# Adding the squares of the mixers' outputs by DMA, moving the first stores to another queue, and reordering ScalarE between two phases

## The chip, the cores and the metric

The kernel runs on one core of a Trainium2 chip. The metric is the device time of one execution in microseconds (us); the median of three runs before the change is 2104.57 us (2098.55 to 2105.23). The engines are called here TensorE (PE in the profile; PEld is its weight load), VectorE (DVE), ScalarE (ACT), GpSimd (POOL) and SyncE (SP). SP and POOL are used mostly to issue DMAs, each on a queue of its own.

## The reference

One step of a hybrid decoder layer in fp32: 2048 prompt tokens and 8 x 4 sample tokens, model width 1024. Cut to what matters:

```
xn   = rms_norm(x, g_mix);  proj = xn @ w_in            # pool 256 | rnn 512 | gate 512 | q 256
o_pool = pool_mixer(...)    o_rnn = gelu(gate) * rg_lru(conv(rnn), ...)    o_xa = cross_attn(q, mk, mv)
mix  = concat(group_rms(o_pool), group_rms(o_rnn), group_rms(o_xa)) * g_out
x    = x + mix @ w_out
x    = x + (gelu(conv(rms_norm(x) @ w_gate)) * (rms_norm(x) @ w_up)) @ w_down
y    = rms_norm(x, g_final)

def group_rms(x):                # over the columns of one mixer's output, for each token
    return x * rsqrt(mean(x * x, -1) + EPS)
```

The change touches how `mean(x * x)` of the three mixers' outputs is formed, where the normalised first tokens are kept for later use, and the first steps of `mix @ w_out`.

## The kernel before, in words

**Layout.** Channels lie on the 128 partitions and tokens along the free dimension. The 2080 tokens are cut into six column sets (`s` = 0 to 5) of 344 or 348 tokens; set 0 holds the sample tokens first. Two sets make a block (`b` = 0 to 2). A product in fp32 quality is made of three matmuls: each operand is split into a high and a low part (`split`, L122 and L123: ScalarE copies the high part, VectorE subtracts it).

**First phase (0 to about 250 us).** For each set the recurrent mixer runs. `g_prep` loads the x columns (L259), scales and splits them (L127, L128) into pairs of tiles `ahr`, `alr`; `g_norm` adds their squares for the token norm; `proj2` (L234) projects; then convolution (L552, L555), gates (`pg` L474, tanh L477), scan (L580), the product with the gate `g` (L597). `g_mix` (L327 on) then normalises the result: ScalarE squares it (L329), `fold` (L352) adds its chunks of 128 channels, TensorE sums the columns with a vector of ones (`rms_stat`, L164, tile `sto`), VectorE takes the reciprocal root (`rsqrt`, L150 to L155), TensorE broadcasts it (L312, tile `bco`), VectorE multiplies (L337) and POOL stores (L339).

**Second phase (about 250 to 504 us).** The same split columns are loaded back from `xhl` (L272) for the pooling and attention mixers of each set. These also end in `g_mix`, with two chunks instead of four (tiles `stp`, `bcp` and `stx`, `bcx`). Behind them the output projection of block 0 begins (`po`).

**Keeping the split columns.** With `keep` given, `g_prep` stores each finished pair to `xhl[s]` in DRAM on POOL's queue (L264). Sets 0 to 5 all use it in the kernel before.

**Squares by DMA.** `fold` and `squares` can add by VectorE or by accumulating DMAs on POOL's queue: `G.dma_start(out=q[:, 0:m], in_=q[:, m:2m], accum_op=ALU.add)`. Before the change only the token norm of sets 1 to 5 (`g_norm`, `dma=s > 0`) takes the DMAs: three in a chain, the first L363 and two of L350, tile `sqr`; their column sum is the tile `str`.

**What sets the order.** The instructions of TensorE and SP run in the order in which the program writes them. Background work (`g_prep`, `g_norm`, `g_mix`, the gates, attention) is written as generators; a planner, `Weave`, lets a clock advance by a fixed cost for each group of matmuls (0.45 for three of them in `proj2`) and takes the next step of a generator when its due time has come. The due times come from the table `W`: in `g_mix` the column sums are written `2.0 + mw * nch` units after the squares, where `mw` is `sq_r`, `sq_p` or `sq_x` and `nch` the number of chunks, and `sq_5` for the last set of the recurrent mixer. In the two first phases VectorE's, ScalarE's and POOL's orders are chosen by the framework; from the passage on they are as written.

**The passage (about 485 to 535 us)** leads to the third phase, in which all products (output projection of blocks 1 and 2, and the gated FFN) are made by a scheme with seven products of half-size pieces for eight. `B0` is the first block's pieces: `B0.hi(i)` and `B0.lo(i)` split piece i (L995, L999). `D[0][s]` are the first pair of outputs, slots s = 0 and 1; `do("hi5", s)` and `do("lo5", s)` split the weights of product 5 (L1055, L1059), `sigma1` adds two raw weight pieces (L1044), `product(0, s, B0)` runs twelve matmuls (L1074), and `post(0, n)` copies the result on ScalarE into another PSUM bank (L1084), on which product 5 goes on adding. TensorE's order of products is 0, 5, 2, 1, 3, 6, 4, each for both slots.

**Third phase (about 535 us to the end).** The change does not touch it.

Of the kernel before, what the change touches and what calls it, by code (L numbers as in the profile page):

```python
# [8 lines left out]
F32 = mybir.dt.float32  # L9
# [7 lines left out]
KD = 8  # L17
# [8 lines left out]
NCOL = [344, 344, 348, 348, 348, 348]  # L26
TOK = [(86, 4)] * 2 + [(116, 3)] * 4
COFF = [0, 344, 688, 1036, 1384, 1732]
NS = 6
# [14 lines left out]
def hybrid_kernel(ctx: ExitStack, tc: tile.TileContext, I, O):  # L44
    nc = tc.nc
# [10 lines left out]

    W = dict(pool_0=12.8, attn_0=1.42, soft0_0=9.0, st_p0=18.9, st_x5=13.5,
             norm_0=9.35, stat_0=2.55, norm_1=17.0, stat_1=4.5, prep_m=2.07, kv=11.0, gate=8.2, norm=20.0, stat=8.5, prep_r=9.7, mix_r=10.2,
             sq_r=1.6, st_r=22.5, mix_5=14.0, sq_5=1.4, st_5=7.0, bc_p=1.0, attn=0.42, soft0=8.5,
             soft1=2.0, soft2=8.5, pv=2.94, pool=10.3, sq_p=1.23, st_p=13.5, sq_x=1.16, st_x=10.5, dq=6.65,  # L60
             dsoft=5.95, dpv=7.01, dout=1.5, mix0=1.19, g2=1.4)

    class Weave:
# [40 lines left out]
    pv = cp.tile([P, NPC], F32, name="pv")  # L104
# [11 lines left out]
    def pcol(name, j):  # L116
        return pv[:, PC[name] + j:PC[name] + j + 1]
# [7 lines left out]
    def split_g(hi, lo, src, g):  # L125

        S.activation(out=hi, in_=src, func=AF.Copy, scale=g)  # L127
        V.scalar_tensor_tensor(out=lo, in0=src, scalar=g, in1=hi.bitcast(F32), op0=ALU.mult, op1=ALU.subtract)  # L128
# [61 lines left out]
    xhl = [dr.tile([P, 2, 8, n], F32, name=f"xhl{s}") for s, n in enumerate(NCOL)]  # L190
# [4 lines left out]
    def x_src(s):  # L195
        return xs[:, COFF[s] * 8:(COFF[s] + NCOL[s]) * 8].rearrange("p (k t) -> p k t", k=8)
# [23 lines left out]
    def big(shape, name):  # L220
        return yp.tile(shape, F32, tag="yh", bufs=2, name=name)
# [4 lines left out]
    def pair(name, n):  # L226

        return [ap.tile([P, 2, n], F32R, tag=t, bufs=8, name=t + name) for t in ("ah", "al")]
# [22 lines left out]
    def g_prep(st, src, n, g, name, parts=2, wait=1.2, keep=None):  # L251

        x = big([P, 8, n], "x" + name)
        st += [x, [pair(f"{name}{k}", n) for k in range(KD // 2)]]
        w = KD // parts
        for k in range(KD):
            if k == 0 or (parts > 2 and k % w == 0):
                for h in range(k, k + w if parts > 2 else KD, w):
                    nc.sync.dma_start(out=x[:, h:h + w, :], in_=src[:, h:h + w, :])  # L259
            hi, lo = (z[:, k % 2, :] for z in st[1][k // 2])  # L260
            split_g(hi, lo, x[:, k, :], pcol(g, k))
            if k % 2 and keep is not None:
                for i in range(2):
                    G.dma_start(out=keep[:, i, k - 1:k + 1], in_=st[1][k // 2][i].bitcast(F32))  # L264
            yield 0.0, wait

    def load_parts(s):

        x = [pair(f"p{s}{k}", NCOL[s]) for k in range(KD // 2)]
        for k in range(KD // 2):  # L270
            for i in range(2):
                nc.sync.dma_start(out=x[k][i].bitcast(F32), in_=xhl[s][:, i, 2 * k:2 * k + 2])  # L272
        return [None, x]
# [30 lines left out]
    def g_stat(sq_list, one, tj, J, rs, name, sd):  # L304

        rms_stat([sq_list], one, tj, J, psC("st" + name), rs, name)
        yield 0.18 * J * len(sq_list), sd

    def g_bcast(rs, n, tj, J, rb, name):
        st = psC("bc" + name)  # L310
        for j in range(J):
            T.transpose(st[:, j * tj:(j + 1) * tj], rs[:tj, j:j + 1].to_broadcast([tj, P]), ident[:tj, :tj])  # L312
        S.activation(out=rb, in_=st[:, 0:n], func=AF.Copy)
        yield 0.1 * J, 1.0
# [10 lines left out]
    def g_mix(o, nch, sqn, one, s, dst, g0, name, mw, sd):  # L325

        n = NCOL[s]  # L327
        tj, J = TOK[s]
        S.activation(out=sqn, in_=o, func=AF.Square)  # L329
        l = fold(sqn, nch)  # L330
        yield 0.0, 2.0 + mw * nch
        rs = cp.tile([P, 8], F32, tag="rs", bufs=2, name="rs" + name)
        yield from g_stat(l, one, tj, J, rs, name, sd)
        rb = kp.tile([P, n], F32, tag="rb2", bufs=1, name="rb" + name)
        yield from g_bcast(rs, n, tj, J, rb, name)
        for c in range(nch):
            V.scalar_tensor_tensor(out=o[:, c, :], in0=o[:, c, :], scalar=pcol("g_out", g0 + c), in1=rb,  # L337
                                   op0=ALU.mult, op1=ALU.mult)
        G.dma_start(out=dst, in_=o)  # L339
# [5 lines left out]
    def fold(q, m, dma=False):  # L345

        while m > 1:
            m //= 2
            if dma:
                G.dma_start(out=q[:, 0:m, :], in_=q[:, m:2 * m, :], accum_op=ALU.add, max_dma_last_dim=8192)  # L350
                continue
            V.tensor_tensor(out=q[:, 0:m, :], in0=q[:, 0:m, :], in1=q[:, m:2 * m, :], op=ALU.add)  # L352
        return [q[:, 0, :]]
# [65 lines left out]
    xq = {0: []}  # L419
    wr = [[]]  # L420
    g = g_load_w(wr[0], I["w_in"][2], "wr0", "a", 2)
    next(g)
    for k, _ in enumerate(g_prep(xq[0], x_src(0), NCOL[0], "g_mix", "r0", 4, keep=xhl[0])):
        if k == 1:
            next(g)
    wv.add(g_norm(xq[0][0], 0, "r0"))
# [77 lines left out]
    for s in range(NS):  # L504
        n = NCOL[s]
        dec = s == 0
# [3 lines left out]
        x = xq.pop(s)  # L510
# [75 lines left out]
        if dec:  # L586
            hs = kp.tile([P, 4, NB], F32, name="hs")
            V.tensor_copy(hs, xc[:, :, 0:ND].rearrange("p c (b t) -> p c b t", t=NT)[:, :, :, NT - 1])
            G.dma_start(out=O["h_s"], in_=hs.rearrange("p c b -> p (c b)"))
            G.dma_start(out=O["conv_s"], in_=xrd.rearrange("p c b t -> p (c b t)"))  # L590
        if s == NS - 1:
            cpo = kp.tile([P, 4, 3], F32, name="cpo")
            for c2 in range(2):
                V.tensor_copy(cpo[:, 2 * c2:2 * c2 + 2, :], xr_prev[c2])
            G.dma_start(out=O["h_p"], in_=h_prev)
            G.dma_start(out=O["conv_p"], in_=cpo.rearrange("p c t -> p (c t)"))
        V.tensor_tensor(out=g, in0=g, in1=xc, op=ALU.mult)  # L597
        wv.add(g_mix(g, 4, xc, 1, s, mix_r[b][:, :, hb, :], 2, f"o{s}",
                     *((W["sq_5"], W["st_5"]) if s == NS - 1 else (W["sq_r"], W["st_r"]))),
               W["mix_5"] if s == NS - 1 else W["mix_r"])  # L600


    x = load_parts(0)
# [18 lines left out]
    def g_pool(s, n, npr, p0, df):  # L622
        b, hb = divmod(s, 2)
        op = tmp("ox", [P, 2, n], f"op{s}")
        for ch in range(2):
            pP = psC(f"pP{s}{ch}")
            T.matmul(pP[:, 0:n], bdp[:, ch, :], df[:, ch, :], start=True, stop=True)
            S.activation(out=op[:, ch, :], in_=pP[:, 0:n], func=AF.Copy, scale=pcol("pscale", ch))
            yield 0.6, 0.0
        yield from g_mix(op, 2, tmp("t", [P, 2, n], f"sqp{s}"), 2, s, mix_p[b][:, 0:2, hb, :], 0, f"p{s}", W["sq_p"], W["st_p" if s else "st_p0"])  # L630
# [23 lines left out]
    def g_attn(s, n, npr, p0, qd, qs):  # L654
# [63 lines left out]
        if p0:  # L718
            yield from g_dec(qd, ox)
        yield from g_mix(ox, 2, tmp("t", [P, 2, n], f"sqx{s}"), 2, s, mix_p[b][:, 2:4, hb, :], 6, f"x{s}", W["sq_x"], W["st_x" if s < NS - 1 else "st_x5"])  # L720

    def g_dec(qd, ox):
# [54 lines left out]
    for s in range(NS):  # L777
        n = NCOL[s]
        tj, J = TOK[s]
        dec = s == 0  # L780
        p0 = ND if dec else 0
        npr = n - p0
        if s:
            x = xq.pop(s)
# [326 lines left out]
    D = []  # L1111
# [191 lines left out]
    def prod(x):  # L1303
        d, y = divmod(x, 14)
        return D[d][y % 2], order[d][y // 2], y % 2
# [90 lines left out]
    B0 = blks[0] = Block("s0", NCOL[2 * stages[0][1]], stages[0][4])  # L1396
# [46 lines left out]
    def do(what, s):  # L1443
        early.pop((what, s))()
# [7 lines left out]
    B0.hi(5)  # L1452
    B0.lo(5)
    for s in range(2):
        D[0][s].w[0] = D[0][s].w0
        do("hi5", s)
        D[0][s].product(0, s, B0)
        D[0][s].post(0, B0.n)
        do("lo5", s)
    do("sigma1", 0)  # L1460
    B0.hi(2)
    B0.lo(2)
    for s in range(2):
        if s:
            do("sigma1", s)
        do("hi2", s)
        do("lo2", s)
# [63 lines left out]
    for x in range(total):  # L1531
# [3 lines left out]
        p, i, s = prod(x)  # L1535
# [9 lines left out]
        k = LASTQ[2 + s]  # L1545
# [125 lines left out]
```

## Time and profile before

| what | value |
|---|---|
| median of three runs | 2104.57 us (2098.55 to 2105.23) |
| the profiled execution's own time | 2102.41 us |
| its span in the profile | 2100.6 us |
| TensorE busy | 2053.6 us (98%) |
| VectorE busy | 1600.9 us (76%) |
| ScalarE busy | 1290.3 us (61%) |
| POOL busy | 111.9 us (5%) |
| mean granted TensorE clock | 0.989 |

The columns of a row differ by view. A row of the timeline is: start (us from the span's start), length (us), engine, line, operation, out<-in by the program's names, shapes, count, and in brackets the idle time before it with what ended it. A row of waits is: who waited, what ended it, then the total in us, the times and the longest. A row of windows is: from:to, length, then busy us of PE, PEld, DVE, ACT and POOL, the granted clock (1.00 is full speed), the share of time in which the DMA engines were busy, and GB/s. A row of a DMA issue gives size and median us from issue to landing; a row of a DMA queue gives packets, MB and share of the 16 engines. A row of the chain of waits is: start, us, what. What ended a wait is inferred; where a row names an instruction that had long been done, it was another.

### The profile page before, as it was taken

The numbers are of one execution on the slowest core, as the hardware profiler recorded it, in microseconds if no ns is written. First come the engines' busy times: TensorE is split into PE (matmuls) and PEld (weight loads), VectorE is DVE, ScalarE is ACT, GpSimd is POOL, SyncE is SP. The second block draws the span as 40 slices with busy tenths as digits, with TensorE's granted clock in tenths as the row PEclk, the third lists the DMA queues.
The fourth block names the chain that finished last, engine by engine and source line by source line (L and its number), as shares of the span: only waits on it lengthen the run. The fifth ranks groups of instructions, "written<-read, shape, count | busy, mean of one in ns | idle before, by whom it ended". The sixth has DMA issues, their size and how long they took to land.

```text
span 2100.6 us, 35349 instructions
## 1 busy us (share of the span) xinstructions
PE 2053.6 (98%) x12996; PEld 1999.6 (95%) x12996; DVE 1600.9 (76%) x2786; ACT 1290.3 (61%) x2322; POOL 111.9 (5%) x151
## 2 busy tenths in 40 slices
PE   8999999999999999999999999999999999999997
PEld 7889898888999999999999999999999999999997
DVE  7786876867988888889897666668778666669775
ACT  7888834544666656566566655556666665557663
POOL 2121000000000000000000000000000000000001
PEclk9999999999999999999999999999999999999998
DMA  8465594236977656668996555677887554677882
GB/s 277 140 196 178 176 311 146 98 121 235 282 207 244 223 196 214 204 233 247 266 276 194 190 174 182 220 259 222 250 246 199 186 182 160 207 269 223 243 225 87
DMA packets 269053, 440.51 MB, mean 210 GB/s; under 512 B 26032, under 2 KB 125712, under 8 KB 268880
## 3 DMA queue, kind: packets, MB, share of 16 engines
q1 hardware_dynamic: 247248, 372.89, 54.1%
q0 software_dynamic: 20400, 63.85, 12.6%
q8 instruction: 102, 1.67, 0.3%
q10 hardware_dynamic: 1232, 1.51, 0.2%
q14 instruction: 71, 0.58, 0.1%
HBM read 297.69 MB, written 139.96 MB: 208 GB/s over the span
## 4 chain that ended last, share of the span: by engine, by line
PE 80%; DVE 6%; DMA 5%; issue 4%; ACT 4%; SPq 0%; POOL 0%; POOLq 0%; ACTq 0%; DVEq 0%
PE bg L1074 10%; PE bu L1074 10%; PE bd L1074 8%; PE ag L1074 7%; PE cg L1074 7%; PE cu L1074 7%; PE au L1074 7%; PE ad L1074 5%; PE cd L1074 5%; PE pq L234 3%; PE bo L1074 2%; PE po L234 2%; PE pu L234 1%; PE co L1074 1%; PE ao L1074 1%
## 5 line engine op out<-in xcount | busy, mean ns | idle before, releaser
L1172 DVE SCALAR_TENSOR_TENSOR cv<-gt,pv,cv 128x696 f32<-128x696 f32 (+2 forms) x144 | 133.1, 925 | 35.1 <-ACT cv L1167 35.1
L1188 DVE TENSOR_TENSOR u<-u,cv 128x696 f32<-128x696 f32 (+1 forms) x72 | 63.3, 879 | 62.5 <-ACT cv L1184 62.5
L1234 POOL DMA_DIRECT2D ys<-cd x32 | 34.8, 1117 | 1365.1 <-ACT cd L1103 918.1
L1074 PE MATMUL bd<-h4s,wt4d 128*128 128x348 f32 (+1 forms) x288 | 71.7, 321 | 4.3 <-DVE cd L1096 4.3
L1074 PE MATMUL ag<-h5s,wt5g 128*128 128x348 f32 (+1 forms) x288 | 74.9, 323 | 0.0
L1074 PE MATMUL cg<-h6s,wt6g 128*128 128x348 f32 (+1 forms) x288 | 74.6, 322 | 0.0
L1074 PE MATMUL cg<-h2s,wt2g 128*128 128x348 f32 (+1 forms) x288 | 74.5, 322 | 0.0
L1074 PE MATMUL bg<-h3s,wt3g 128*128 128x348 f32 (+1 forms) x288 | 74.5, 321 | 0.0
L1074 PE MATMUL bg<-h1s,wt1g 128*128 128x348 f32 (+1 forms) x288 | 74.5, 321 | 0.0
L1074 PE MATMUL cu<-h6s,wt6u 128*128 128x348 f32 (+1 forms) x288 | 74.5, 322 | 0.0
L1074 PE MATMUL bg<-h4s,wt4g 128*128 128x348 f32 (+1 forms) x288 | 74.5, 321 | 0.0
L1074 PE MATMUL ag<-h0s,wt0g 128*128 128x348 f32 (+1 forms) x288 | 74.4, 321 | 0.0
L1074 PE MATMUL au<-h0s,wt0u 128*128 128x348 f32 (+1 forms) x288 | 74.4, 320 | 0.0
L1074 PE MATMUL bu<-h4s,wt4u 128*128 128x348 f32 (+1 forms) x288 | 74.4, 320 | 0.0
L1074 PE MATMUL bu<-h3s,wt3u 128*128 128x348 f32 (+1 forms) x288 | 74.4, 320 | 0.0
L1074 PE MATMUL bu<-h1s,wt1u 128*128 128x348 f32 (+1 forms) x288 | 74.4, 320 | 0.0
L1074 PE MATMUL au<-h5s,wt5u 128*128 128x348 f32 (+1 forms) x288 | 74.3, 321 | 0.0
L1074 PE MATMUL cu<-h2s,wt2u 128*128 128x348 f32 (+1 forms) x288 | 74.3, 321 | 0.0
L1074 PE MATMUL bd<-h3s,wt3d 128*128 128x348 f32 (+1 forms) x288 | 71.9, 321 | 1.6 <-ACT t6d L1092 1.6
L1074 PE MATMUL cd<-h6s,wt6d 128*128 128x348 f32 (+1 forms) x288 | 72.2, 322 | 0.0
L1074 PE MATMUL ad<-h5s,wt5d 128*128 128x348 f32 (+1 forms) x288 | 71.5, 321 | 0.0
L1074 PE MATMUL bd<-h1s,wt1d 128*128 128x348 f32 (+1 forms) x288 | 71.5, 321 | 0.0
(561 smaller groups left out, 7493.1 us busy)
## 6 DMA issues: line engine op xcount, KB each, us to landing
hs<-u SPq DMA_DIRECT2D x24, 696.0 KB, 4.0
ys<-cd POOLq DMA_DIRECT2D x20, 696.0 KB, 11.0
wr22g<-in_w_gate_dram SPq DMA_DIRECT2D x36, 256.0 KB, 4.1
wr11g<-in_w_gate_dram SPq DMA_DIRECT2D x36, 256.0 KB, 4.9
wr12g<-in_w_gate_dram SPq DMA_DIRECT2D x36, 256.0 KB, 5.0
wr22u<-in_w_up_dram SPq DMA_DIRECT2D x36, 256.0 KB, 6.5
wr11u<-in_w_up_dram SPq DMA_DIRECT2D x36, 256.0 KB, 6.6
wr12u<-in_w_up_dram SPq DMA_DIRECT2D x36, 256.0 KB, 6.6
```

The lines of the kernel that those rows point to most:

```text
L234: T.matmul(o, w_[:, ks], z, start=(k == 0 and i == 0), stop=(k == nk - 1 and i == 2))
L1074: T.matmul(pt[:, 0:n], w[:, w_, ks_(k)], blk.hl[i][a_][:, k, :], start=(i in (0, 2) and k == m == 0), stop=(k == 3 and m == 2), skip_group ...
L1172: V.scalar_tensor_tensor(out=cv[:, z0:nn], in0=gt[:, z0 + t:nn + t], scalar=pcol("fcw", 3 * f + t), in1=cv[:, z0:nn], op0=ALU.mult, op1=AL ...
L1188: V.tensor_tensor(out=u, in0=u, in1=k["cv"][:, i, 0:nn], op=ALU.mult)
L1234: at[N + 14 + 1 + s].append(lambda j=2 * d + s, k=ks[s]: G.dma_start(out=flat(ys[b][j]), in_=qv(k["c"], n), accum_op=ALU.add, max_dma_last ...
```

## The change

It has four parts. The folds of the squares in `g_mix` go by accumulating DMA on POOL's queue for sets 0 to 4 (set 5 stays on VectorE). The entries `sq_r`, `sq_p` and `sq_x` of the planner's table become 3.2, so that the column sums are written later; `sq_p` and `sq_x` hold for set 5 too. The stores of set 0's split columns to `xhl[0]` no longer go out from `g_prep` on POOL's queue, pair by pair; eight DMAs on SP's queue do it, written behind the scan of set 0, which in SP's order is behind the loads of set 1's columns. In the passage both slots' product-5 weights are split first, then both products 0 are written, and the two copies of `post` follow, the second one behind the split of piece 2.

```diff
--- before.py
+++ after.py
@@ -56,8 +56,8 @@
...
-             sq_r=1.6, st_r=22.5, mix_5=14.0, sq_5=1.4, st_5=7.0, bc_p=1.0, attn=0.42, soft0=8.5,
-             soft1=2.0, soft2=8.5, pv=2.94, pool=10.3, sq_p=1.23, st_p=13.5, sq_x=1.16, st_x=10.5, dq=6.65,
+             sq_r=3.2, st_r=22.5, mix_5=14.0, sq_5=1.4, st_5=7.0, bc_p=1.0, attn=0.42, soft0=8.5,
+             soft1=2.0, soft2=8.5, pv=2.94, pool=10.3, sq_p=3.2, st_p=13.5, sq_x=3.2, st_x=10.5, dq=6.65,
...
@@ -327,7 +327,7 @@
         S.activation(out=sqn, in_=o, func=AF.Square)
-        l = fold(sqn, nch)
+        l = fold(sqn, nch, s < NS - 1)
         yield 0.0, 2.0 + mw * nch
...
@@ -420,7 +420,7 @@
-    for k, _ in enumerate(g_prep(xq[0], x_src(0), NCOL[0], "g_mix", "r0", 4, keep=xhl[0])):
+    for k, _ in enumerate(g_prep(xq[0], x_src(0), NCOL[0], "g_mix", "r0", 4)):
...
@@ -588,6 +588,10 @@
             G.dma_start(out=O["conv_s"], in_=xrd.rearrange("p c b t -> p (c b t)"))
+        if dec:
+            for k in range(KD // 2):
+                for i in range(2):
+                    nc.sync.dma_start(out=xhl[0][:, i, 2 * k:2 * k + 2], in_=x[1][k][i].bitcast(F32))
         if s == NS - 1:
...
@@ -1452,14 +1456,16 @@
     B0.hi(5)
     B0.lo(5)
     for s in range(2):
+        do("hi5", s)
+        do("lo5", s)
+    for s in range(2):
         D[0][s].w[0] = D[0][s].w0
-        do("hi5", s)
         D[0][s].product(0, s, B0)
-        D[0][s].post(0, B0.n)
-        do("lo5", s)
     do("sigma1", 0)
+    D[0][0].post(0, B0.n)
     B0.hi(2)
     B0.lo(2)
+    D[0][1].post(0, B0.n)
     for s in range(2):
         if s:
             do("sigma1", s)
```

## The prediction, made before the change was run

> **What bounds the kernel now.** I read the page first, then TensorE's waits, then windows around each wait, then the engines' timelines there.
>
> ```profile
> span 2100.6 us, 35349 instructions
> PE 2053.6 (98%) x12996; PEld 1999.6 (95%) x12996; DVE 1600.9 (76%) x2786; ACT 1290.3 (61%) x2322; POOL 111.9 (5%) x151
> ```
>
> TensorE is busy for 98% of the span and the change takes no matmul away. So only TensorE's idle time, 47.0 us, and the time in which its clock is granted at half rate can be won. Its list of waits says which of them the change can reach:
>
> ```profile
> PE pg L474 <- DVE xc L555: 5.1, 2, 2.7
> PE bcr L312 <- DVE rsx L155: 3.2, 1, 3.2
> PE pS L671 <- ACT rbp L313: 2.1, 1, 2.1
> PE str L164 <- ACT i L477: 1.6, 1, 1.6
> PE bo L1074 <- ACT h1s L995: 1.5, 1, 1.5
> PE str L164 <- DMA xhl<-ahr: 1.0, 1, 1.0
> ```
>
> Each of these is small. But a long one costs twice, for the clock falls behind it (windows; the column after POOL is the granted clock, then DMA share and GB/s):
>
> ```profile
> 27.40:30.80 3.40, 3.40 (x14) 3.40 (x13) 3.26 (x8) 2.91 (x4) 0.00 (x0) 0.51 0.96 378
> 153.70:160.50 6.80, 6.80 (x25) 5.58 (x24) 4.21 (x26) 3.21 (x4) 1.08 (x2) 0.50 0.96 306
> 235.60:239.00 3.40, 3.40 (x11) 2.44 (x12) 3.40 (x7) 3.34 (x6) 0.00 (x0) 0.51 0.25 61
> 522.40:529.20 6.80, 5.61 (x18) 5.24 (x19) 6.80 (x9) 6.80 (x11) 0.00 (x0) 0.50 0.89 271
> ```
>
> A stretch of 3.4 us at 0.5 costs 1.7 us of matmuls, one of 6.8 us costs 3.4. They follow the waits of 3.2 (bcr), 1.6 (str), 2.7 (pg) and 1.5 us (bo, with more behind it); the wait of 1.0 us has none. So about 1.5 us is where a wait begins to cost double.
>
> **The change part by part. (1) The first stores** (`keep=xhl[0]`, eight of 344 KB) leave POOL's queue and come on SP's, behind the loads of the next columns.
>
> ```profile
> xhl<-ahr POOLq DMA_DIRECT2D x4, 344.0 KB, 7.4
> q0 software_dynamic: 507, 2.17, 52.9%
> q1 hardware_dynamic: 1754, 1.78, 52.4%
> 13.82 9.64 DMA st_wr<-in_w_in_dram
> 21.65 0.16 DVE L153 SCALAR_TENSOR_TENSOR thr<-rsx 86x4 f32<-86x4 f32 x1
> 24.57 1.23 DVE L123 TENSOR_TENSOR l_wr<-st_wr,h_wr 128x1024 fp32r<-128x1024 f32 x1 [2.76 <-ACT h_wr L122]
> 26.21 0.48 PE L312 MATMUL bcr<-ident,rsx 86*128 86x86 f32 x4 [3.21 <-DVE rsx L155]
> ```
>
> The queue rows are for 13 to 23 us: POOL's stores moved 2.17 MB while the loads moved 1.78, on full engines (52.9 + 52.4%). In that time one weight load took 9.64 us. VectorE stood at its split (24.57) in the middle of the reciprocal root that bcr needs. The stores' 2.17 MB are 5.7 us at the 378 GB/s of the row above, so without them the load, now there at 23.46, is there by about 17.8 (an estimate). VectorE's order stays, so after 21.65 come the split (1.23) and two operations of 0.16: bcr can start at 23.5, and TensorE is free at 26.21 - 3.21 = 23.0. Won: 2.7 us, and the half-rate stretch of 1.7 behind it: 4.4.
>
> What is late next: the same 2.8 MB (8 x 344 KB; the row shows one of the two halves) now come after the load of the second columns, beside the accumulating DMAs for the second columns' sum.
>
> ```profile
> 26.20 0.90 SPq L259 DMA_DIRECT2D xr<-in_x_dram  x2
> 30.00:36.00 6.00, 6.00 (x38) 6.00 (x37) 5.45 (x15) 4.13 (x6) 1.08 (x2) 0.93 0.57 227
> 36.00:46.00 10.00, 9.83 (x50) 6.74 (x49) 9.59 (x29) 9.12 (x19) 4.00 (x6) 1.00 0.93 242
> 46.53 0.86 POOL L350 DMA_DIRECT2D sqr<-sqr  x1 [3.21 <-DMA sqr<-sqr]
> 51.42 0.70 PE L164 MATMUL str<-ones,sqr 128*86 128x1 f32 x8
> sqr<-sqr POOLq DMA_DIRECT2D x1, 688.0 KB, 5.5
> sqr<-sqr POOLq DMA_DIRECT2D x1, 344.0 KB, 4.1
> sqr<-sqr POOLq DMA_DIRECT2D x1, 172.0 KB, 3.3
> ```
>
> SP issues that load at 26.20, then nothing until the third columns' load, so the eight issues (0.45 us each by this row) hold nobody up and go out at once. 2.8 MB at 378 GB/s are 7.4 us of all engines; from 30 to 46 us only 6 x 0.43 + 10 x 0.07 = 3.3 us of them are free. Up to 4.1 us of transfer push the chain that now lands at 46.53 + 3.3 = 49.8. It starts some 2.7 us earlier too (its load's issue comes behind the buffer that the split of 24.57 frees), so it lands between 47.1 and 51.2, while TensorE, 4.4 us earlier, comes at 47.0. A wait of 0 to 4.2 us; I take 1.8 with a third of a half-rate stretch (0.6). **Part 1: -2.0; ends -4.4 and, with the whole wait and a whole stretch, +1.5.** The Trainium skill's page DMA: Bandwidth & Descriptors, section Queues, rings and completion order, says that each DMA engine goes round the queues it has work for, a packet at a time; the equal shares above agree, and by that rule the stores on another queue gain no bandwidth and take half of it from the chain while they last.
>
> **(2) VectorE loses the adds** of the mixers' squares for five of the six column sets.
>
> ```profile
> L352 DVE TENSOR_TENSOR xc<-xc x12: 508/697/884, 71.7 to 265.2; 128x696 f32<-128x696 f32 x4, 128x348 f32<-128x348 f32 x4, 128x688 f32<-128x688 f32 x2, 128x344 f32<-128x344 f32 x2
> 225.68 0.87 DVE L352 TENSOR_TENSOR xc<-xc 128x696 f32<-128x696 f32 x1
> 229.66 0.87 DVE L543 TENSOR_TENSOR xr<-pr,rbr 128x696 f32<-128x696 f32 x1
> 232.77 3.03 DVE L555 SCALAR_TENSOR_TENSOR xc<-xr,pv,xc 128x348 f32<-128x348 f32 x6
> 235.46 1.31 PE L474 MATMUL pg<-xc,bdg 64*128 64x348 f32 x3 [2.72 <-DVE xc L555]
> ```
>
> Ten of the recurrent adds (0.70 mean) and ten of 0.51 for pooling and attention: 7.0 + 5.1 = 12.1 us of VectorE. Nearly all lies where TensorE does not wait for it. One place does: before 235.46 two adds (0.87 and 0.51) stand just ahead of the chain L543, L555. L543 waits for its product anyway, but the 232.77 - 229.66 - 0.87 = 2.2 us of other work behind it can move forward by 1.4. The wait falls from 2.72 to 1.3, around the point where the clock falls (half of 1.7). **-2.2; ends 0** (VectorE's order keeps the gap) **and -4.4** (wait and stretch both gone).
>
> **(3) POOL gets 20 accumulating DMAs**, two chained ones per recurrent set, one per pooling and attention set. The column sums come later for it: 2.0 + 3.2 x 4 = 14.8 planner units behind the squares instead of 8.4, and 8.4 instead of 4.4 (a unit is about a us: `proj2` ticks 0.45 for three matmuls). By the rows above two hops take 4.1 + 3.3 and two issues of 0.88, 9.2 us, and one takes 4.2: covered by 5.6 and 4.2 us. The planner fills the place with other matmuls, so the move costs TensorE nothing. At the end of the phase the last attention sum also goes 4 units later without a DMA; matmuls of the output projection cover it.
>
> The price is elsewhere: POOL's queue also carries the norm's chain, and TensorE waits for that.
>
> ```profile
> 150.29 0.89 POOL L350 DMA_DIRECT2D sqr<-sqr  x1 [3.44 <-DMA sqr<-sqr]
> 153.54 1.12 PE L164 MATMUL str<-ones,sqr 128*116 128x1 f32 x6 [1.64 <-ACT i L477]
> ```
>
> The last hop is issued at 150.29 and takes about 3.1 to 3.3, so it lands at 153.5: the wait of 1.64 is for this DMA, whatever the row names. The wait of 1.0 us (str) is the same chain at 78.55. The new folds are issued between its first and last hop. POOL has room (it idles 3.44 us before this hop), so an issue delays at most 0.9 us, but the bytes share the queue: from 688 to 172 KB the landing falls by 2.2 us for 516 KB, so the 516 KB of the two folds cost 0 to 2.2 us per stage. Four stages: 0 to 8.8, and up to two more half-rate stretches (3.4). I take 0.55 per stage, nearer to the idle queue than to a full one, and half a stretch. **+3.0; ends 0 and +12.2.** In the second phase the moved sums change which buffer is free when: 0, ends -2 and +2 (the wait pS is 2.1).
>
> **(4) ScalarE in the passage.** hi5 of both slots now comes ahead of the copies of the first products (post, L1084).
>
> ```profile
> 508.63 0.45 ACT L1084 ACTIVATE bo<-ao 128x348 f32<-128x348 f32 x1 [1.70 <-PE ao L1074]
> 511.48 0.63 ACT L1055 ACTIVATE wt5o<-wr12o 128x512 fp32r<-128x512 f32 x1 [2.40 <-DMA wr12o<-in_w_out_dram]
> 512.39 1.35 ACT L995 ACTIVATE h2s<-q12s 128x1392 fp32r<-128x1392 f32 x1
> 510.31 0.32 PE L1074 MATMUL ao<-h5s,wt5o 128*128 128x348 f32 x1
> 521.40 0.43 PE L1074 MATMUL bo<-h1s,wt1o 128*128 128x348 f32 x1 [1.50 <-ACT h1s L995]
> 524.25 0.95 PE L1074 MATMUL bo<-h1s,wt1o 128*128 128x348 f32 x2 [0.55 <-DVE wt1o L1059]
> ```
>
> The second hi5 waits for its weights until 511.48. The copy now done at 509.1 stands behind it and ends at 512.6; the product of 510.31 needs it: TensorE waits 2.3 us more. The other copy comes behind h2 (1.35) and ends at 514.4, about when the second slot's product needs it. But from 519.9 (521.40 - 1.50) to 524.25 TensorE runs two matmuls (0.43 each) and waits about 3.5 us for h1, l1 and wt1. Their chain on ScalarE and VectorE begins with h2, which starts at 512.6 instead of 512.4, and has the second copy (0.45) behind it: it moves by 0.2 to 0.6, I take 0.3. The 2.3 us come out of that wait. **+0.3; ends +2.3** (not absorbed) **and -3.4** (the shorter wait at 521 no longer drops the clock).
>
> **The sum**: -2.0 - 2.2 + 3.0 + 0 + 0.3 = -0.9 us. The profiled execution took 2102.41 us (span 2100.6, 1.8 around it); that gives 2101.5. The median of the three runs, 2104.57, lies 2.2 above it, so the forecast for a median is **2103.7**.
>
> **Rivals.** *Faster, 2096.1*: the start keeps its 4.4, the wait at 235 goes with its stretch (4.4), the folds cost nothing, the passage +0.3: -8.5. For it: DMA share is only 0.25 behind 235.6 and POOL idles. Against: the start's stores must go somewhere. *Slower, 2112.9*: the folds' bytes sit ahead of the norm's chain in POOL's queue at all four stages, str waits 2.2 us more each time, twice with a new stretch: +12.2, less 4.2 of parts 1 and 2, and 0.3: +8.3. It decides from about 1.7 us per stage on, where the sum passes 6.3. For it: this chain already ends TensorE's waits (78.55, 153.54). Against: the hops' waits on POOL are latency more than bytes. *The stores only move the stall* (the page's rule above, told as this kernel's mechanism): the 4.4 of the start come back as a wait at the second str plus a stretch, part 1 is +1.5, sum +2.6: 2107.2, no measurable change.
>
> **How the numbers follow.** About 0.3% (6.3 us) is what a measurement can tell here. Forecast 0.35, stores only move the stall 0.13, faster 0.29, slower 0.23. So faster 0.29, same 0.48, slower 0.23. The range goes from 2 us beyond the faster case to the slower one: 2094 to 2113; the forecast's own is 2099 to 2109. The Trainium skill's page TensorE: Matmul & The Clock Gate, Part 1, says that the window that drops the clock runs free of the kernel; by it any stretch above may come or stay away from run to run, which no row here can show and no term uses.
>
> **What would show it.** Right: bcr's wait under 1 us and no low clock at 27 us; str of the second columns waits instead; pg's wait at 235 halves; a new wait of about 2 us at the product of hi5 and a shorter one at h1s. Wrong: str waits over 2 us in several stages (slower), or no wait at the second str (faster).

## The result and the profile after

The kernel became slower: 2115.3 us (median of 4 runs, 2113.8 to 2117.5) against 2102.3 (median of 4, 2098.6 to 2105.2), a ratio of 1.0060 with a 95% interval of 1.0044 to 1.0076. That is 12.6 us, from 9 to 16. The forecast was 2103.7, and its range ended at 2113. The profiled execution of the changed kernel took 2117.5 us, the longest of its four; before's took 2102.4.

The page of the changed kernel, span and busy times:

```profile
span 2115.6 us, 35396 instructions
PE 2062.2 (97%) x12996; PEld 2008.8 (95%) x12996; DVE 1593.5 (75%) x2766; ACT 1292.0 (61%) x2322; POOL 125.7 (6%) x163
```

VectorE lost its 20 adds (2786 to 2766 operations) and 7.4 us of busy time, where the prediction counted 12.1. TensorE has the same 12996 matmuls, but is busy 8.6 us longer and idle 53.4 us instead of 47.0. Its list of waits (who waited, what ended it, total, times, longest):

```profile
PE str L164 <- DMA sqr<-sqr: 4.9, 2, 3.4
PE pg L474 <- DVE xc L555: 4.1, 2, 2.3
...
PE bcp L312 <- DVE rsp L155: 3.5, 1, 3.5
PE str L164 <- ACT r L492: 3.2, 1, 3.2
...
PE stp L164 <- DMA sqp<-sqp: 1.6, 1, 1.6
...
PE ao L1078 <- ACT bo L1088: 1.4, 1, 1.4
...
PE bcr L312 <- DVE rsx L155: 0.4, 1, 0.4
```

The wait of bcr fell from 3.2 to 0.4 us, as forecast. New are str of the second columns (3.2), bcp (3.5), stp (1.6) and ao (1.4); of pg's waits, the one that should have halved is gone, and another of 2.3 us has come. Where they stand on TensorE:

```profile
53.01 1.30 PE L164 MATMUL str<-ones,sqr 128*86 128x1 f32 x8 [3.18 <-ACT r L492]
...
233.15 1.03 PE L474 MATMUL pg<-xc,bdg 64*128 64x348 f32 x4 [2.32 <-DVE xc L555]
...
244.05 0.86 PE L474 MATMUL pg<-xc,bdg 64*128 64x348 f32 x4
...
370.56 0.71 PE L164 MATMUL stp<-ones,sqp 128*116 128x1 f32 x3 [1.56 <-DMA sqp<-sqp]
...
450.23 0.84 PE L312 MATMUL bcp<-ident,rsp 116*128 116x116 f32 x3 [3.49 <-DVE rsp L155]
...
525.16 0.43 PE L1078 MATMUL ao<-h5s,wt5o 128*128 128x348 f32 x1 [1.36 <-ACT bo L1088]
```

The pg at 244.05 is the one of 235.46 before. The pg at 233.15 is the pair ahead of it (the first of the sixth columns), which before waited 0.2 us.

And windows of the same execution, where the low clock of before stood at 27 us and behind the new waits (the column before the DMA share is the granted clock):

```profile
27.30:30.70 3.40, 2.77 (x18) 2.51 (x17) 3.40 (x8) 1.65 (x3) 0.00 (x0) 1.00 1.05 318
52.80:59.60 6.80, 6.59 (x27) 6.62 (x28) 3.36 (x14) 3.37 (x3) 0.00 (x0) 0.50 0.94 336
...
233.70:237.10 3.40, 3.40 (x15) 2.93 (x12) 3.40 (x5) 2.86 (x5) 0.88 (x1) 0.50 0.71 167
448.70:455.60 6.90, 5.37 (x23) 5.31 (x23) 5.21 (x15) 4.91 (x12) 1.50 (x2) 0.51 0.54 174
370.20:377.10 6.90, 6.54 (x27) 6.13 (x27) 3.47 (x11) 3.05 (x10) 0.00 (x0) 0.51 0.66 212
```

The stretch at 27 us is gone; the new ones behind str, bcp and stp are of 6.8 us each, twice as long as the one saved. Three others are shorter than before: those that began at 153.7, 283.4 and 522.4 us lasted 6.8 us each, and now they begin at 162.0, 291.7 and 537.5 and last 3.4. Up to 560 us the half-rate time is 37.5 us instead of 30.7, which is 3.4 us of matmuls more.

### The profile page after: what moved, and what is told of

Same layout as the page of the kernel before. It is cut to its first block, busy times and chain, and to the rows that moved or that the text cites. A ratio compares the mean times of both kernels' runs of the same rounds, so it can differ in the third digit from the quotient of the medians.

```text
span 2115.6 us, 35396 instructions
## 1 busy us (share of the span) xinstructions
PE 2062.2 (97%) x12996; PEld 2008.8 (95%) x12996; DVE 1593.5 (75%) x2766; ACT 1292.0 (61%) x2322; POOL 125.7 (6%) x163
## 4 chain that ended last, share of the span: by engine, by line
PE 76%; issue 9%; DMA 5%; DVE 5%; ACT 3%; POOL 1%; SPq 0%; POOLq 0%; DVEq 0%; ACTq 0%
PE bg L1078 10%; PE bu L1078 10%; PE bd L1078 8%; PE ag L1078 7%; PE cg L1078 6%; PE cu L1078 6%; PE au L1078 6%; PE ad L1078 5%; PE cd L1078 5%; PE pq L234 2%; PE bo L1078 2%; PE po L234 2%; DMA sqr<-sqr 1%; PE co L1078 1%; PE ao L1078 1%
## 5 line engine op out<-in xcount | busy, mean ns | idle before, releaser
L1078 PE MATMUL bd<-h4s,wt4d 128*128 128x348 f32 (+1 forms) x288 | 72.9, 326 | 3.9 <-DVE cd L1100 3.9
L1078 PE MATMUL ag<-h5s,wt5g 128*128 128x348 f32 (+1 forms) x288 | 74.9, 323 | 0.0
L1078 PE MATMUL cg<-h6s,wt6g 128*128 128x348 f32 (+1 forms) x288 | 74.6, 322 | 0.0
L1078 PE MATMUL cg<-h2s,wt2g 128*128 128x348 f32 (+1 forms) x288 | 74.5, 322 | 0.0
L1078 PE MATMUL bg<-h3s,wt3g 128*128 128x348 f32 (+1 forms) x288 | 74.5, 321 | 0.0
L1078 PE MATMUL bg<-h1s,wt1g 128*128 128x348 f32 (+1 forms) x288 | 74.5, 321 | 0.0
L1078 PE MATMUL cu<-h6s,wt6u 128*128 128x348 f32 (+1 forms) x288 | 74.5, 322 | 0.0
L1078 PE MATMUL bg<-h4s,wt4g 128*128 128x348 f32 (+1 forms) x288 | 74.5, 321 | 0.0
L1078 PE MATMUL ag<-h0s,wt0g 128*128 128x348 f32 (+1 forms) x288 | 74.4, 321 | 0.0
L1078 PE MATMUL au<-h0s,wt0u 128*128 128x348 f32 (+1 forms) x288 | 74.4, 320 | 0.0
L1078 PE MATMUL bu<-h3s,wt3u 128*128 128x348 f32 (+1 forms) x288 | 74.4, 320 | 0.0
L1078 PE MATMUL bu<-h4s,wt4u 128*128 128x348 f32 (+1 forms) x288 | 74.4, 320 | 0.0
L1078 PE MATMUL bu<-h1s,wt1u 128*128 128x348 f32 (+1 forms) x288 | 74.4, 320 | 0.0
L1078 PE MATMUL au<-h5s,wt5u 128*128 128x348 f32 (+1 forms) x288 | 74.3, 321 | 0.0
L1078 PE MATMUL cu<-h2s,wt2u 128*128 128x348 f32 (+1 forms) x288 | 74.3, 321 | 0.0
L1078 PE MATMUL bd<-h3s,wt3d 128*128 128x348 f32 (+1 forms) x288 | 71.9, 321 | 1.9 <-ACT t6d L1096 1.9
L1078 PE MATMUL cd<-h6s,wt6d 128*128 128x348 f32 (+1 forms) x288 | 73.3, 326 | 0.0
L1078 PE MATMUL ad<-h5s,wt5d 128*128 128x348 f32 (+1 forms) x288 | 71.5, 321 | 0.0
L1078 PE MATMUL bd<-h1s,wt1d 128*128 128x348 f32 (+1 forms) x288 | 71.5, 321 | 0.0
```

The lines of the kernel that those rows point to most:

```text
L1078: T.matmul(pt[:, 0:n], w[:, w_, ks_(k)], blk.hl[i][a_][:, k, :], start=(i in (0, 2) and k == m == 0), stop=(k == 3 and m == 2), skip_group ...
```

## The experiments

The theory going in, A: each part pays its own price where the trace of the changed kernel shows a new wait, the stores at str, the folds and places at stp and bcp, the passage none. Its rivals are the forecast's own sum (D), its slower rival (B), the places instead of the DMAs (C) or the reverse (F), and a delay that is taken up again (E); G and H came after the first four runs.

Each kernel was timed in five rounds beside the kernel before, four kernels to a chip. "Ratio" is to the kernel before, with its 95% interval; 0.1% is 2.1 us. The differences in us below are worked out from the ratios; those of the medians differ from them by up to 1.4 us. One run of a kernel differs from the next by up to 10 us (before: 2097 to 2107), so the medians decide and a single trace only shows where things happen.

### The parts one by one

**Stores only** (`stores_only`): of the diff only `keep=xhl[0]` taken out and the eight `nc.sync.dma_start` put in.

> Only part 1: the first columns' eight stores on SP's queue, nothing else changed. Theory A (each part pays its own price where the trace of the changed kernel shows it): the wait of bcr falls from 3.2 us to about 0.4, and str of the second columns waits some 3 us for an accumulating DMA whose first hop takes about 10 us instead of 5.5 beside the stores, with a half-rate stretch of 6.8 us behind it: -1.8 at the start, +6.4 there, so 3 to 5 us above the kernel before (2105 to 2107). Theory D (the prediction's step): a wait of 1.8 us at str, -2.0 in all, 2100. Theory E (the delay at the second columns is taken up again by slack of the later stages): within 1 us of the kernel before.

Measured: 2106.0, ratio 1.0020 (1.0010 to 1.0029): 4.2 us slower, theory A. On TensorE str of the second columns waits 4.07 us:

```profile
53.47 0.71 PE L164 MATMUL str<-ones,sqr 128*86 128x1 f32 x4 [4.07 <-issue]
```

The cause is seen in the changed kernel's trace. SP issues the eight stores one behind the other, behind the load of the second columns, just ahead of the first hop on POOL:

```profile
25.79 0.58 SPq L594 DMA_DIRECT2D xhl<-ahr  x1
...
33.06 0.32 SPq L594 DMA_DIRECT2D xhl<-alr  x1
...
34.85 0.90 POOL L363 DMA_DIRECT2D sqr<-sqr  x1 [1.18 <-ACT sqr L361]
```

Its DMA queues (packets, MB, share of the engines) in 34 to 46 us, and that hop (KB, us to landing):

```profile
q0 software_dynamic: 496, 2.18, 59.3%
q1 hardware_dynamic: 815, 1.97, 43.3%
...
sqr<-sqr POOLq DMA_DIRECT2D x1, 688.0 KB, 9.9
```

The hop takes 9.9 us where the same 688 KB took 5.5 before, and in these 12 us the stores' queue (q1) moves nearly as many bytes as POOL's (q0), which carries the hop and, as before, some stores of the second columns. The Trainium skill's page DMA: Bandwidth & Descriptors, section Queues, rings and completion order, says that an engine goes round the queues it has work for; the trace agrees (1.97 MB against 2.18).

**Folds only** (`folds_only`): `l = fold(sqn, nch, s < NS - 1)` and the three entries of `W`.

> Only parts 2 and 3: 20 accumulating DMAs for the mixers' squares and the column sums placed later; stores and passage as before. Theory A: 6 to 9 us slower, of which 5 to 7 lie in the second phase (stp of the third columns waits about 1.6 us for its accumulating DMA, bcp of the fifth columns about 3.5 us for VectorE's reciprocal root, a half-rate stretch behind each) and 1 to 2 in the first. Theory B (the prediction's slower rival: the folds' bytes ahead of the norm's chain): about 8 us slower, all in the first phase, str waits 2.2 us longer at each of four stages. Theory D (the prediction's sum of these parts): +0.8 us, no stage with a new wait.

Measured: 2108.95, ratio 1.0035 (1.0020 to 1.0049): 7.4 us slower, in theory A's range. The waits that it named in the second phase are there (bcp 2.9, stp 0.9 us), but the next kernel shows that its split between the phases does not explain the loss.

**Passage only** (`passage_only`): the passage's part of the diff alone.

> Only part 4: ScalarE's order in the passage. Theories A and D agree within what can be measured: -1 to +0.5 us, with a new wait of 1.4 to 2.3 us at the product of hi5 and shorter ones at h1s, l1s and wt1. Rival: the new wait is not taken up and brings its own half-rate stretch, +2.3 to +4.

Measured: 2102.98, ratio 1.0005 (0.9995 to 1.0015): no difference that can be told from none. The product of hi5 waits 1.7 us, h1s 1.0 instead of 1.5.

**Places only** (`place_only`): the three entries of `W`, and no accumulating DMA.

> Only the three planner costs of the column sums (sq_r, sq_p, sq_x) at their later values; VectorE still adds the squares, no accumulating DMA is added, stores and passage as before. Theory C (the new places alone make the later waits, because VectorE's reciprocal root comes behind other work when its sum comes later): 4 to 7 us slower with bcp of the fifth columns waiting some 3 us. Theory F (the DMAs make the waits, the place costs nothing, as the prediction said): within 1 us of the kernel before, no new wait at bcp or stp.

Measured: 2097.69, ratio 0.9976 (0.9965 to 0.9987): **5 us faster** than before. Both theories fall. Theory C named the right new wait, bcp at the fifth columns (3.3 us here), but the places gain more than it costs. So the 20 DMAs with the same places cost 0.9976 to 1.0035: 12.4 us, where the forecast had 0.8 for parts 2 and 3 together.

The parts add up: 4.2 + 7.4 + 1.1 = 12.7 against 12.6 us for the whole change. What remains is where 12.4 us of the DMAs come from.

### What the DMAs cost

**Recurrent folds, and pooling and attention folds, apart** (`rec_folds`, `pa_folds`): all later places, and

```diff
-        l = fold(sqn, nch)
+        l = fold(sqn, nch, s < NS - 1 and nch == 4)   # rec_folds; nch == 2 in pa_folds
```

> The later places for all column sums, accumulating DMAs only for the recurrent mixer (ten of the twenty); pooling and attention add on VectorE; stores and passage as before. TensorE's order is that of the kernel with the later places alone (2097.7). Theory G (the ten recurrent folds share POOL's queue with the norm's chain, which lands about 0.9 us later at each of four stages, and the order that the scheduler writes for ScalarE turns at the fifth columns): 8 to 10 us above the later places alone, 2106 to 2108; str waits 1 to 2 us at four stages, pg waits 2.5 us near 224 us. Theory H (every added DMA costs alike): half of the difference, about 2103.

> The later places for all column sums, accumulating DMAs only for pooling and attention (the other ten); the recurrent mixer adds on VectorE; stores and passage as before. Theory G: within 2 us of the later places alone (2097 to 2100), one new wait of about 1 us at stp of the third columns, where the DMA runs beside eight loads. Theory H (every added DMA costs alike): about 2103.

Measured: `rec_folds` 2109.1, ratio 1.0032 (1.0020 to 1.0043), 11.8 us above the places alone; `pa_folds` 2101.32, ratio 0.9995 (0.9985 to 1.0006), 4.0 us above them. The recurrent folds carry most of it, as theory G says; the other ten cost 4.0 where it allows 2 us, but each of these differences is known only to some 3 us. The two prices sum to 15.8, not 12.4; with that uncertainty it is not a contradiction.

The recurrent folds' first price is the norm's chain. On TensorE, str of the fifth columns in `place_only`:

```profile
151.04 0.74 PE L164 MATMUL str<-ones,sqr 128*116 128x1 f32 x6 [0.52 <-ACT r L477]
```

and in `folds_only`:

```profile
154.50 0.74 PE L164 MATMUL str<-ones,sqr 128*116 128x1 f32 x6 [1.62 <-DMA sqr<-sqr]
```

Over the four stages that have folds it waits 0, 0.1, 0.5 and 0 us without the DMAs and 2.0, 1.1, 1.6 and 1.1 with them: 5.2 us more. The first of the four is no clean case, though: in `place_rec`, below, str of the third columns waits 3.7 us without any such DMA. The other three are 3.2 us. The last hop's issue (KB, us to landing) in `place_only`:

```profile
sqr<-sqr POOLq DMA_DIRECT2D x1, 174.0 KB, 3.0
```

and in `folds_only`, with the fold that shares the queue with it:

```profile
sqr<-sqr POOLq DMA_DIRECT2D x1, 348.0 KB, 3.8
xc<-xc POOLq DMA_DIRECT2D x1, 348.0 KB, 5.1
sqr<-sqr POOLq DMA_DIRECT2D x1, 174.0 KB, 4.1
```

The last hop takes 1.1 us longer, and the first fold 5.1 us where the chain's hop of the same 348 KB takes 3.8.

**ScalarE's order held** (`folds_order`). TensorE's order in `folds_only` is that of `place_only`, instruction by instruction; but VectorE's and ScalarE's, which the framework chooses, are not. In the fifth columns ScalarE of the kernel before takes the square root (L496) first and then the gelu (L577):

```profile
209.71 1.37 ACT L496 ACTIVATE xc<-xc 128x1392 f32<-128x1392 f32 x1 [0.37 <-DVE xc L495]
211.09 1.28 ACT L577 ACT_TABLE_LOAD   x1
212.39 1.37 ACT L577 ACTIVATE g<-g 128x1392 f32<-128x1392 f32 x1
```

In the changed kernel, as in `folds_only`, they are turned round:

```profile
216.05 1.37 ACT L577 ACTIVATE g<-g 128x1392 f32<-128x1392 f32 x1
217.44 1.28 ACT L496 ACT_TABLE_LOAD   x1
218.73 1.37 ACT L496 ACTIVATE xc<-xc 128x1392 f32<-128x1392 f32 x1
...
227.55 1.37 ACT L329 ACTIVATE xc<-g 128x1392 f32<-128x1392 f32 x1 [3.31 <-DVE g L601]
228.82 1.04 ACT L361 ACTIVATE xm<-xm 128x1024 f32<-128x1024 f32 x1
229.77 1.23 ACT L552 ACTIVATE xc<-xr,pv 128x348 f32<-128x348 f32 x2
```

and VectorE waits for the root:

```profile
220.13 1.61 DVE L497 TENSOR_TENSOR i<-i,xc 128x1392 f32<-128x1392 f32 x1 [3.57 <-ACT xc L496]
...
225.86 1.60 DVE L601 TENSOR_TENSOR g<-g,xc 128x1392 f32<-128x1392 f32 x1
```

The scan and the product L601 come late, so the square L329 comes late too, and ScalarE runs it and L361 ahead of L552, which the convolution of the next columns needs; pg waits at its end (233.15). To test that, a dependency holds the gelu back:

```diff
+        if s == 4:
+            zb = kp.tile([P, 1], F32, name="zb")
+            S.activation(out=zb, in_=xc[:, 0, 0:1], func=AF.Copy, scale=0.0)
+            S.activation(out=g, in_=g, func=AF.Gelu_apprx_tanh, bias=zb)
```

> All 20 accumulating DMAs and the later places, and in the fifth columns alone the gelu gets a bias of zero that ScalarE works out from the square root's result (one copy of one column, times zero), so that it can't come ahead of the square root as it does with the DMAs; stores and passage as before. If the turned order on ScalarE makes the waits of pg near 224 and 232 us (the scan begins 8 us later than without the DMAs): those waits and the half-rate stretch go, 3 to 5 us below the DMAs with the later places (2108.95), about 2105. If the order is only a bystander: 2108 to 2110.

Measured: 2102.65, ratio 1.0003 (0.9993 to 1.0014), against 1.0035 without the dependency: 6.7 us less (some 4 either way), somewhat more than expected. ScalarE's and VectorE's orders differ from those of `folds_only` only from the fifth columns' gelu on (about 209 us). In its trace that pg starts without a wait:

```profile
226.43 0.85 PE L474 MATMUL pg<-xc,bdg 64*128 64x348 f32 x4
```

The traces agree on the size. From str to bco of the sixth columns TensorE takes 87.2 or 87.3 us in the three with the turned order (the changed kernel, `folds_only`, `rec_folds`), 81.9 and 82.0 in the two with the order held (this one and `repaired`, below), and 83.3 in `place_only`.

So of the 12.4 us, about 6.7 are an order that no line of the change mentions. The other 5.7 are of the size of str's waits (3.2 to 5.2) and stp's (0.9) together. By the estimate in the table at the end, though, some 4 us of this rest are clock and 2 the waits themselves, each known to 2 or 3 us.

### The stores, and the two causes together

**Stores one stage later** (`place_late`): the later places, VectorE's adds, and the eight stores written behind the load of the third columns.

```diff
             wv.tick(0.0)
+            if dec:
+                x0 = x
+            if s == 1:
+                for k in range(KD // 2):
+                    for i in range(2):
+                        nc.sync.dma_start(out=xhl[0][:, i, 2 * k:2 * k + 2], in_=x0[1][k][i].bitcast(F32))
```

> The later places, VectorE's adds, and the first columns' eight stores on SP's queue one stage later than in the change: behind the load of the third columns instead of the second. If the stores' bytes beside the first hop of the second columns' sum made the wait of 3 to 4 us at str: the hop takes 5.5 us again, bcr waits 0.4 us and str of the second columns not at all, 1 to 3 us below the later places alone (2095 to 2097), unless the splits of the third columns, which need the stored buffers, come late: then str of the third columns waits and the time is 2098 to 2102.

Measured: 2096.28, ratio 0.9975 (0.9961 to 0.9989). The mechanism is confirmed; the first hop is back at its length:

```profile
sqr<-sqr POOLq DMA_DIRECT2D x1, 688.0 KB, 5.5
```

and on TensorE bcr starts at 23.5 and str of the second columns finds its sum ready:

```profile
23.50 0.48 PE L312 MATMUL bcr<-ident,rsx 86*128 86x86 f32 x4 [0.37 <-DVE rsx L155]
...
48.10 0.70 PE L164 MATMUL str<-ones,sqr 128*86 128x1 f32 x8
```

The trace is 2.0 us ahead of `place_only`'s there, but the ratio (0.9975 beside 0.9976) can't tell such a gain from none.

**The change with both causes taken out** (`repaired`): the change, with the stores as in `place_late` and the gelu as in `folds_order`.

> The whole change with two causes taken out: the first columns' eight stores come on SP's queue one stage later (behind the load of the third columns), and the gelu of the fifth columns is held behind the square root as before; all 20 accumulating DMAs, the later places and ScalarE's order in the passage stay. If these two are what the change loses by (about 4 and 6 us of its 13): 2101 to 2105, within 0.15% of the kernel before. If the waits only move on, or the DMAs cost as much by themselves: 2108 or more.

Measured: 2100.59, ratio 0.9994 (0.9983 to 1.0005). From 1.0060 that is 13.9 us, where the two causes by themselves were 4.2 and 6.7: within the uncertainty they account for the loss. What stays of the change is then worth nothing measurable: the later places' gain and the DMAs' own price cancel within it. The norm's chain is still not free: str of the third columns waits 3.2 us in this trace, 1.0 in that of `place_late`; what the folds and what the stores do to it there was not separated.

### Which places gain

**Recurrent sums only, pooling and attention sums only** (`place_rec`: `sq_r=3.2`; `place_pa`: `sq_p=3.2, sq_x=3.2`; VectorE's adds).

> Only the recurrent sums (sq_r) placed later, VectorE adds all squares, all else as before. If the gain of the later places (5 us) is made in the first phase, where the sum of the next columns' norm now comes ahead of the mixer's, and part of it is lost again at bcp of the fifth columns (3.3 us, its sum comes too late for VectorE there): no wait at bcp, 2093 to 2097. If the places of pooling and attention make the gain: 2101 to 2103.

> Only the sums of pooling and attention (sq_p, sq_x) placed later, VectorE adds all squares, all else as before. By the first reading of the run before: the wait of about 3 us at bcp of the fifth columns with its half-rate stretch comes, 2 to 5 us slower than the kernel before, 2104 to 2106. By the second reading: about 2098.

Measured: `place_rec` 2096.18, ratio 0.9979 (0.9968 to 0.9990), 4.4 us faster, no wait at bcp; `place_pa` 2105.5, ratio 1.0022 (1.0011 to 1.0033), 4.6 us slower, with that wait:

```profile
439.36 0.51 PE L312 MATMUL bcp<-ident,rsp 116*128 116x116 f32 x3 [3.27 <-DVE rsp L155]
```

Where the later recurrent sum gains is seen on VectorE in `place_only`:

```profile
225.52 3.03 DVE L555 SCALAR_TENSOR_TENSOR xc<-xr,pv,xc 128x348 f32<-128x348 f32 x6
...
229.66 1.07 DVE L337 SCALAR_TENSOR_TENSOR g<-g,pv,rbo 128x348 f32<-128x348 f32 x2
```

The scaling of the earlier columns' output (L337) comes behind the convolution that the pg of 235.46 waits for; before, all four stood ahead of it, at 227.3 to 229.3, with L555 from 232.77. That pg waits 0.5 us instead of 2.7. And str of the fifth columns waits 0.5 instead of 1.6. What this wins is the clock: before, half-rate stretches of 6.8 and 3.4 us followed the waits at str and pg, and none follows there in the five traces that have the later recurrent sum and leave its adds on VectorE (`place_only`, `place_rec`, `place_late`, `rec_late`, `pa_folds`). Why bcp is late is seen on VectorE in the changed kernel:

```profile
444.10 0.15 DVE L168 TENSOR_SCALAR vvp<-stp 116x3 f32<-116x3 f32 x1
...
448.10 1.23 DVE L123 TENSOR_TENSOR l_wo<-st_wo,h_wo 128x1024 fp32r<-128x1024 f32 x1 [1.12 <-ACT h_wo L122]
```

The column sum ran at 434.7 to 435.4, but its reciprocal root begins at 444.1, behind 9 us of VectorE's other work, and a weight split that waits for ScalarE stands in its middle. Before, the sum ran at 422.3 and its root began at 423.0. The changed kernel is some 10 us behind there, so the sum itself moved little; `place_pa`, which is level with the kernel before until then, shows it. There the sum runs at 424.0, 1.7 us later, and the root begins 10.5 us later:

```profile
433.48 0.15 DVE L168 TENSOR_SCALAR vvp<-stp 116x3 f32<-116x3 f32 x1
```

What moved is the root's place in VectorE's order.

One thing does not add up: -4.4 and +4.6 give nothing, and the two together (`place_only`) gain 5.0. The bcp wait is in `place_only` too, and a half-rate stretch of 3.4 us follows it in both traces. By the table at the end the 4.6 us are mostly clock. Why they do not show in `place_only` is not settled.

**The gains together** (`rec_late`): `sq_r=3.2` and the stores as in `place_late`.

> The recurrent sums later, VectorE's adds, and the first columns' eight stores on SP's queue behind the load of the third columns: what of the change gained by itself, with the stores where they met no norm chain. If the gains add (5 us or more of the places, 2 us of the start): 2091 to 2096, 6 to 10 us below the kernel before. If the stores' gain is lost at a later wait: as the recurrent places alone.

Measured: 2094.45, ratio 0.9972 (0.9961 to 0.9982): 5.9 us faster than the kernel before and about 18 below the changed one, the lowest median here. Beside `place_rec` alone (0.9979) the stores' part is within the uncertainty.

## Why the prediction was wrong

The forecast was 0.9 us below the profiled execution, and the kernel came out 12.6 us slower. Of the 13.5 us between them, 6.2 are part 1's (+4.2 instead of -2.0) and 6.6 are parts 2 and 3's (+7.4 instead of +0.8).

**Part 1 (-2.0, ends -4.4 and +1.5; measured +4.2, 2.1 to 6.1).** The start was right: bcr's wait 0.4, no low clock at 27 us, and 23.5 for bcr is what `place_late` shows. (In the changed kernel's own trace TensorE came to the first str 1.6 us later, so that less was won.) The step that failed is "it lands between 47.1 and 51.2". It landed at 52.8. The stores' push was nearly sized, 4.4 us in the first hop against at most 4.1; but the chain started 1.2 us earlier (34.85 instead of 36.07), not 2.7. Then 1.8 was taken from a range of 0 to 4.2 although the rule just quoted, equal shares for both queues, said that the whole push comes; and the stall behind it was priced at 0.6, while 6.8 us at half rate are 3.4. Here 3.2 + 3.4 less 1.8 at the start (pg of the first columns at 37.7 instead of 39.5) = 4.8. "The stores only move the stall" was the right rival, with too small a price.

**Part 2 (-2.2; gained, but not by the adds).** The wait at 235.46 went, even wholly; but it goes to 0.5 in `place_only` too, where VectorE keeps its adds. It was the later place that moved L337 away. "The work behind L543 can move forward by 1.4" was the wrong lever, and where the recurrent folds went to DMAs the framework wrote another order, with a wait of 2.3 us at the pg before.

**Part 3 (+3.0, ends 0 and +12.2).** Two terms failed and one was left out. The norm's chain: 0.55 us per stage were taken, and about 1.1 measured at the three clean ones, inside the 0 to 2.2; "nearer to the idle queue" was the wrong choice of end. "The move costs TensorE nothing" failed in both directions: recurrent sums -4.4, pooling and attention sums +4.6 alone. In the second phase "0, ends -2 and +2" missed the late root at bcp and stp's wait for a DMA beside the loads. Left out altogether, and the largest: the turned order on ScalarE, 6.7 us. The rule "VectorE's order stays" stood in part 1 and was carried over unasked, though only TensorE's and SP's orders are written by the program.

**Part 4 (+0.3; measured +1.1, -1.1 to +3.2).** Right within what can be told: a new wait of 1.4 us (2.3 was forecast) and a shorter one at h1s.

**Where a wait costs double.** The prediction set this at about 1.5 us and priced part 2 by it. The length of the wait alone does not decide: pg's 2.72 us at 235.46 was followed by half rate before, and the same 2.72 us at 238.0 in `stores_only` was not. The last section shows what the traces say in its place.

**The slower rival** (2112.9) had the nearest time, but its mechanism, 2.2 us per stage, was 3 to 5 of the 12.6 us. Its sign, "str waits over 2 us in several stages", came at two stages, and neither speaks for it: 3.2 us at the second columns is the stores, and at the third (3.4) the chain of hops took 14.2 us from first issue to last landing, against 14.1 before.

## What to carry to other kernels

When an edit takes instructions off an engine whose order a scheduler chooses, compare the orders of all such engines before pricing the edit: a pair that swaps far from the edit can cost more than all that was counted. A bulk store moved to another queue does not leave the chain it was meant to free; here its queue moved 1.97 MB beside the 2.18 of the chain's, and the chain's first hop took 9.9 us instead of 5.5. So put it where no chain waits. And test the parts of a bundle alone: here a side setting, the later place of one sum, was the only part with a gain that can be measured.

## What the runs showed of the hardware

A wait of 3.2 us in the third phase, which the change does not touch (`bd`, L1074, now L1078), stands in both traces with the same idle time, but the clock falls behind it in only one.

In every trace here the half-rate stretches begin on one grid of 3.413 us. In the kernel before they begin at 27.4, 71.8, 153.7, 235.6, 283.4 and 522.4 us; the steps between these are 13, 24, 24, 14 and 70 times 3.413. Where the grid begins differs from trace to trace. Windows of the kernel before, laid on its grid:

```profile
1102.63:1106.05 3.42, 1.87 (x12) 1.58 (x11) 3.42 (x5) 0.97 (x3) 0.00 (x0) 1.00 0.28 99
1106.05:1109.46 3.41, 1.75 (x11) 1.75 (x12) 3.41 (x6) 3.35 (x4) 0.00 (x0) 1.00 0.00 0
1109.46:1112.87 3.41, 3.41 (x24) 3.41 (x23) 3.41 (x6) 1.96 (x4) 1.19 (x2) 1.00 0.58 159
```

and of the changed one, on its own:

```profile
1117.80:1121.20 3.40, 0.79 (x5) 0.79 (x6) 3.40 (x5) 2.75 (x4) 0.00 (x0) 0.99 0.00 0
1121.20:1124.60 3.40, 3.40 (x14) 3.40 (x13) 3.40 (x6) 1.86 (x3) 0.19 (x1) 0.50 0.32 109
```

Before, the grid cuts the wait in two: TensorE is busy for 1.87 and 1.75 us of two windows, and the clock stays. In the changed kernel most of the wait lies in one window, with 0.79 us busy, and the clock halves behind it: 14 matmuls instead of 24. The Trainium skill's page TensorE: Matmul & The Clock Gate, Part 1, says that the window runs free of the kernel; these rows agree. Counted over the 14 traces from 10 us on, a full-rate window with TensorE busy under 1.5 us was followed by half rate 59 times of 59, one with 1.5 to 2.5 us 26 times of 94, and one with more never (of 8182). The ends of matmuls are modelled, so these bounds are rough. So a wait of about 3 us costs 1.7 or 3.4 us more in some executions, and a single trace with or without such a stretch says little of a kernel's time.

The runs show how much this is. Each has its span and its mean granted clock on record, and span times (1 - clock) estimates what the low clock took. In the 31 runs of the kernel before that were timed beside the first four kernels, the spans spread by 2.8 us (standard deviation); less this estimate, by 1.4. The means over each kernel's runs, less those of the kernel before on the same chip, in us (known to about 2 for the clock, 1 to 2 for the rest):

| kernel | clock | rest |
|---|---|---|
| `stores_only` | +2.1 | +0.6 |
| `folds_only` | +1.1 | +5.0 |
| `folds_order` | -0.4 | +1.3 |
| `place_only` | -4.3 | -1.0 |
| `place_rec` | -4.5 | -0.2 |
| `place_pa` | +2.8 | +0.7 |
| `rec_late` | -3.7 | -3.0 |
| `repaired` | -1.5 | 0.0 |

The gain of the later recurrent sums is clock nearly alone. The turned order on ScalarE is mostly time by itself (3.7 of the 5.2 us between `folds_only` and `folds_order`). And the stores moved to where no chain waits show in the rest: -3.0 beside the -0.2 of `place_rec`.
